# Weighted sums of modulation rows in a streaming-encoder block: products by ScalarE in place, sums by adding transfers on GpSimd's queue

## The chip, the cores and the metric

The kernel runs on one core of one Trainium2 chip. The metric is the device time of one execution in microseconds (us), here the median of three runs. The engines are TensorE (PE in the profile, PEld for its weight loads), VectorE (DVE), ScalarE (ACT), GpSimd (POOL) and SyncE (SP, which only issues transfers). Each takes its own list of instructions in order and waits at its head for semaphores of the others. 16 DMA engines move the data.

## The reference, cut to what matters

One residual block over x of 1024 tokens by 1024 channels: a mixer (four heads of a gated delta rule in chunks of 64, and a short gated convolution), then a SwiGLU, each behind a norm that a vector c modulates.

```python
c_act = jax.nn.silu(c)
mod = (c_act @ w_ada[l] + b_ada[l])[:, None, :]
shift1, scale1, gate1, shift2, scale2, gate2 = jnp.split(mod, 6, axis=-1)
h = rms_norm(x, norm1_w[l]) * (1.0 + scale1) + shift1
x = x + gate1 * hybrid_mixer(h, ...)
h = rms_norm(x, norm2_w[l]) * (1.0 + scale2) + shift2
x = x + gate2 * swiglu(h, w_gate[l], w_up[l], w_down[l])
return rms_norm(x, norm_f_w)
```

`w_ada` is 1024 by 6144, so `mod` is six rows of 1024 numbers. shift1 and scale1 (rows 0 and 1) are needed at the start and are made in another way. The late rows are 2 (gate1), 3 (shift2), 4 (scale2) and 5 (gate2); the change touches the sums of rows 2, 3 and 4, and the first product of row 5.

## The kernel before, in words

Everything is float32. Large matrix products are done as three float32r products of high and low parts, 128 by 128 weights times 128 by 512 data. The run has two parts. In the first, to about 470 us, all projections of the mixer, the delta rule and half of the output projection are made; in the second, the rest of the output projection and the SwiGLU (with a Strassen-like scheme).

The order of the first part is not written by hand. Every step is a task (`sim.spawn`, with a priority), and a planner (`class Sim`, L302) runs the tasks in a model of the engines with costs for each kind of instruction (`cost`, L371), takes at each point the task that could start first, and writes its instruction next. The result is one fixed list per engine. So a change of a cost or of an instruction gives another order for the whole of the first part from there on. Dense projections (`fill`, the tile `acc`) have the lowest priority and fill PE between the steps of the delta rule; their weights come through `raw` buffers and are split into parts `u`.

Late modulation rows are made by `ada_rows(b, ch)` (L988), one half row of 512 at a time. A half row has eight blocks kk of 128 rows of `w_ada`. For each block a buffer `raw` (there are five, shared with the loads of weights) is taken and loaded by SP, and VectorE multiplies it by the column kk of `c_act`, one number per partition, and adds it to `ac` (the tile `aacc`): a `tensor_scalar` for the first block (L998), a `scalar_tensor_tensor` for the seven others (L1000). What is left is a sum over the 128 partitions: `aacc` is split into a high and a low part (a cast by ScalarE or VectorE and a subtraction by VectorE), and two PE matmuls with a matrix of ones (the tile `ada`) put the sum into every partition of a PSUM bank.

`ada` (L1026) calls this for both halves of rows 2, 3 and 4, one after the other, without a buffer of its own (`get` is None, so `row` is true). There is one buffer `aacc`, so a half row begins when the one before has been split. For rows 3 and 4 the result is multiplied by an identity into `diag`, which uses the buffer of `aacc` too, and reduced to columns `mod_c`. `gate5` (L1015) makes row 5 later and passes buffers, so `row` is false there.

GpSimd has little to do in this part: per-head inverse roots (`rk`, `ro`), and the clearing of `A` (an array V that the recurrence of the delta rule fills: in each step matmuls `K`, `O` and `A`) before each of its steps.

Of the kernel before, what the change touches and what calls it, by code (L numbers as in the profile page):

```python
# [12 lines left out]
AF = mybir.ActivationFunctionType  # L13
ALU = mybir.AluOpType
# [37 lines left out]
def kernel(  # L52
# [25 lines left out]
    class Ordered:  # L78
# [18 lines left out]
    PE, DVE, ACT, POOL, SP = (Ordered(n, e) for n, e in (  # L97
        ("pe", nc.tensor), ("dve", nc.vector), ("act", nc.scalar), ("pool", nc.gpsimd), ("sp", nc.sync)))
# [7 lines left out]
    def nm(s):  # L106
        n_id[0] += 1
        return f"{s}_{n_id[0]}"

    xs, outs = x[0], out[0]  # L110
# [9 lines left out]
    class Banks:  # L120
# [3 lines left out]
        def get(self, name="ps"):  # L124
            b = self.ids[self.i % len(self.ids)]
            self.i += 1
            return psp.tile([P, HT], F32, name=nm(name), tag=f"b{b}")
# [61 lines left out]
    def dma(out, in_):  # L189
        SP.dma_start(out=out, in_=in_)  # L190
# [19 lines left out]
    c_act = cst.tile([P, KB], F32, name="c_act", tag="c_act")  # L210
# [91 lines left out]
    class Sim:  # L302
# [18 lines left out]
        def free(self, t):  # L321
            res, i = self.owner.pop(t.tensor.name)
            res.slots.append((max([a[4] for a in self.acc.get(t.tensor.name, [])] + [0.0]), i))
            res.slots.sort()
# [46 lines left out]
        def cost(self, eng, op, a, k):  # L371
            outs, ins = [], []
            pos = [v for v in a if hasattr(v, "tensor")]
            if "out" in k:
                outs.append(k["out"])
            else:
                outs.append(pos.pop(0))
            ins += pos
            for n, v in k.items():
                if n != "out" and hasattr(v, "tensor"):  # L380
                    (outs if n == "accum_out" else ins).append(v)
            o = outs[0]
            n = o.free_size()
            table = None
            if eng == "pe":
                if op == "transpose":
                    busy = 0.107
                else:
                    fast = ins[1].dtype == F32R
                    busy = max(n * 0.000443, 0.107) if fast else max(n * 0.00168, 0.224)  # L390
                lat = busy + 0.30
            elif op == "dma_start":
                busy, lat = 0.44, None
            elif eng == "act":
                big = max([n] + [v.free_size() for v in ins])
                busy = 0.15 + (0.1 if hasattr(k.get("scale"), "tensor") else 0.0) + big * 0.0007 + (0.19 if "accum_out" in k else 0.0)
                lat = busy + 0.25
                func = [v for v in a if isinstance(v, type(AF.Silu)) and v in (AF.Silu, AF.Exp, AF.Ln)] if op == "activation" else []
                if func:
                    table = str(func[0]).split(".")[-1]  # L400
            elif eng == "pool":
                busy = 1.1 if op == "tensor_tensor" else 0.5
                lat = busy + 0.15
            else:
                big = max([n] + [v.free_size() for v in ins])
                sb = all(v.space != PSUM for v in outs + ins)
                if op == "memset":
                    busy = 0.08 + n * 0.0005
                elif sb and op in ("tensor_copy", "tensor_scalar"):
                    busy = 0.08 + n * 0.00062  # L410
                else:
                    busy = 0.08 + big * 0.00104 + (0.05 if op == "scalar_tensor_tensor" else 0.0)
                if "accum_out" in k:
                    busy += 0.1
                lat = busy + 0.15
            return outs, ins, busy, lat, table
# [147 lines left out]
    def bank(res, name):  # L564
        return res.tile(psp, [P, HT], F32, name)

    def gt(tag, shape=(P, 4, P), dtype=F32):
        return GP[tag].tile(gp, list(shape), dtype, tag)

    def raw(shape=(P, HT), dtype=F32):  # L570
        return raws.tile(wst, list(shape), dtype, "raw")
# [10 lines left out]
    def esplit(src, hi, lo):  # L582
        ecopy(hi, src)
        DVE.tensor_tensor(lo, src, hi.bitcast(F32), ALU.subtract)

    def mm(out_, lhsT, rhs, start=True, stop=True):
        PE.matmul(out_, lhsT, rhs, start=start, stop=stop)
# [400 lines left out]
    def ada_rows(b, ch, ac=None, get=None):  # L988
        if ac is None:
            ac = wst.tile([P, HT], F32, name=nm("aacc"), tag="aacc", bufs=1)  # L990
        row = get is None
        get = get or raw
        c0 = b * D + ch * HT
        for kk in range(KB):
            r = get()
            dma(r, wada[kk * P:(kk + 1) * P, c0:c0 + HT])
            if kk == 0:
                DVE.tensor_scalar(ac, r, c_act[:, 0:1], None, ALU.mult)  # L998
            else:
                DVE.scalar_tensor_tensor(ac, r, c_act[:, kk:kk + 1], ac, ALU.mult, ALU.add)  # L1000
            free(r)
        hl = [raw(dtype=F32R) if row else gt("Tt", (P, HT), F32R) for _ in range(2)]
        esplit(ac, hl[0], hl[1])
        if not row:
            return hl
        ps = bank(chb, "ada")
        mm(ps, ones_r, hl[0], True, False)
        mm(ps, ones_r, hl[1], False, True)
        for t in hl:
            free(t)  # L1010
        return ps
# [3 lines left out]
    def gate5(ch):  # L1015
        sim.wait(lambda: len(us0) == KB and len(us1) == KB and "row" in done)
        if 5 not in gates:
            g = gates[5] = wst.tile([P, D], F32, name=nm("gate"), tag="gate", bufs=1)
            dma(g, b_ada[0, 5 * D:6 * D].partition_broadcast(P))
        ac = gt("A", (P, HT)) if ch else None  # L1020
        g5[ch] = ada_rows(5, ch, ac, (lambda: gt("Tt", (P, HT))) if ch else raw)
        done.add(("g5", ch))
        if ch:
            free(ac)

    def ada():  # L1026
        sim.wait(lambda: 1 in sc_)
        g = wst.tile([P, D], F32, name=nm("gate"), tag="gate", bufs=1)
        dma(g, b_ada[0, 2 * D:3 * D].partition_broadcast(P))
        for ch in range(2):  # L1030
            ps = ada_rows(2, ch)
            DVE.tensor_tensor(g[:, ch * HT:(ch + 1) * HT], g[:, ch * HT:(ch + 1) * HT], ps, ALU.add)
            free(ps)
        gates[2] = g
        for b in (3, 4):
            for ch in range(2):
                ps = ada_rows(b, ch)
                j = (b - 3) * 8 + ch * 4
                diag = wst.tile([P, 4, P], F32, name=nm("diag"), tag="aacc", bufs=1)
                DVE.tensor_tensor(diag, v3(ps, 4), bc1(ident, 4), ALU.mult)  # L1040
                free(ps)
                DVE.tensor_reduce(mod_c[:, j:j + 4], diag, mybir.AxisListType.X, ALU.add)
        DVE.tensor_tensor(mod_c, mod_c, bac[:, 24:40], ALU.add)
        DVE.tensor_copy(b2c, mod_c[:, 0:8])
        DVE.scalar_tensor_tensor(s2c, mod_c[:, 8:16], 1.0, n2c, ALU.add, ALU.mult)
        DVE.tensor_tensor(db2, b2c[:, 4:8], b2c[:, 0:4], ALU.subtract)
        done.add("mods")
# [1348 lines left out]
```

## Time and profile before

| what | value |
|---|---|
| median of three runs | 1159.26 us |
| range of the three runs | 1158.74 to 1159.27 us |
| profiled execution, first to last instruction (span) | 1158.3 us |
| PE, DVE, ACT, POOL busy in the span | 1148.2, 961.4, 565.6, 62.3 us |
| first and last start of a VectorE step on `aacc` | 113.0 and 465.8 us |
| DMA engines' busy share, 100 to 470 us | 0.49 |

Of the profiled execution its span is known; its own time is among the three runs, whose median lies 1.0 us above the span.

In the rows of groups the parts are: source line, engine, operation, the tile written and the tiles read, shapes, count, then busy time in us and the mean of one in ns, then the engine's idle time just before these instructions with what ended most of it. Nearly all instructions of the first part carry L448, the planner's line. In the rows of waits the numbers are us in total, times, and the longest. In the rows of the chain and of the timeline they are start and length in us. In the rows of DMA issues the last number is the median from issue to landing in us.

### The profile page before, as it was taken

What the parts mean: (1) busy time and instruction counts of PE and PEld (TensorE: products, weight loads), DVE (VectorE), ACT (ScalarE), POOL (GpSimd) and SP (SyncE); (2) the same over time, 40 slices, a digit from 0 to 9 for tenths busy, and PEclk for the clock granted to TensorE, in tenths of its full rate; (3) what the DMA queues carried; (4) which work ended last, traced back from release to release, by engine and by line L of the source; (5) the groups of instructions that cost most, each with busy time, mean ns of one, the idle gap of its engine ahead of it and who ended that gap; (6) DMA issues with size and microseconds to landing.
All of it is one profiled execution on the core that took longest, in us unless ns stands there. A gap on an engine that the chain in (4) does not pass through costs nothing.

```text
span 1158.3 us, 16873 instructions
## 1 busy us (share of the span) xinstructions
PE 1148.2 (99%) x5682; PEld 967.1 (83%) x5682; DVE 961.4 (83%) x1820; ACT 565.6 (49%) x1244; POOL 62.3 (5%) x100
## 2 busy tenths in 40 slices
PE   8999999999999999999999999999999999999997
PEld 7888888988888988888888888888888888888886
DVE  7899988999988898669987778877887798688676
ACT  6678732559634543346434443434434455443344
POOL 2110100001101001100000000000000000000002
PEclk9999999999999999999999999999999999999999
DMA  9824456534225546432564457545654599869403
GB/s 363 324 76 143 117 166 174 182 120 138 88 66 164 165 158 210 169 92 72 173 218 163 138 191 231 171 137 175 232 192 143 174 333 394 309 207 337 144 30 146
DMA packets 127544, 209.19 MB, mean 181 GB/s; under 512 B 20577, under 2 KB 45153, under 8 KB 127457
## 3 DMA queue, kind: packets, MB, share of 16 engines
q1 hardware_dynamic: 122080, 204.90, 52.8%
q10 hardware_dynamic: 5376, 3.21, 0.9%
q8 instruction: 45, 0.74, 0.3%
q14 instruction: 43, 0.34, 0.1%
HBM read 153.01 MB, written 55.05 MB: 180 GB/s over the span
## 4 chain that ended last, share of the span: by engine, by line
PE 94%; DVE 3%; ACT 1%; DMA 1%; issue 0%; ACTq 0%; DVEq 0%
PE acc L89 36%; PE acc L448 25%; PE dn L89 17%; PE o L89 4%; PE o L448 3%; PE tr L89 1%; PE K L448 1%; PE A L448 1%; DVE xo L90 1%; PE ab L448 1%; PE w L448 1%; PE u L448 1%; PE kk L448 1%; PE qk L448 1%; DMA raw<-in_w_out_dram 0%; DVE raw L448 0%
## 5 line engine op out<-in xcount | busy, mean ns | idle before, releaser
L448 PE MATMUL acc<-h,u 128*128 128x512 f32 x1200 | 297.9, 397 | 0.0
L448 PEld LDWEIGHTS acc<-h,u 128*128 128x128 f32 x1200 | 220.0, 188 | 42.5 <-issue 0.5
L89 PE MATMUL acc<-h,hl 128*128 128x512 f32 x576 | 135.1, 390 | 0.0
L89 PE MATMUL acc<-T,hl 128*128 128x512 f32 x552 | 130.8, 390 | 0.0
L89 PEld LDWEIGHTS acc<-h,hl 128*128 128x128 f32 x576 | 107.4, 188 | 21.9
L89 PEld LDWEIGHTS acc<-T,hl 128*128 128x128 f32 x552 | 102.4, 188 | 20.4
L90 DVE TENSOR_TENSOR xo<-xo,dn 128x512 f32<-128x512 f32 x84 | 57.0, 684 | 42.3 <-PE dn L89 34.6
L89 PE MATMUL acc<-h,u 128*128 128x512 f32 (+1 forms) x480 | 91.8, 341 | 0.0
L89 PE MATMUL dn<-h,h 128*128 128x512 f32 x396 | 90.7, 389 | 0.0
L89 PEld LDWEIGHTS acc<-h,u 128*128 128x128 f32 x480 | 78.3, 189 | 11.7
L89 PEld LDWEIGHTS dn<-h,h 128*128 128x128 f32 x396 | 74.3, 188 | 15.4
L90 DVE TENSOR_TENSOR cc<-cc,acc 128x512 f32<-128x512 f32 x66 | 41.4, 645 | 32.0 <-PE acc L89 32.0
L448 ACT CAST u<-raw 128x512 fp32r<-128x512 f32 x58 | 35.9, 621 | 56.9 <-PE acc L448 55.1
L448 DVE TENSOR_TENSOR u<-raw,u 128x512 fp32r<-128x512 f32 x82 | 56.1, 685 | 4.0 <-ACT u L448 3.5
L89 PE MATMUL acc<-T,u 128*128 128x512 f32 x240 | 56.0, 389 | 0.0
L448 DVE SCALAR_TENSOR_TENSOR cv<-pr,cols_a,cv 128x512 f32<-128x512 f32 x72 | 53.8, 756 | 0.3
L89 PEld LDWEIGHTS acc<-T,u 128*128 128x128 f32 x240 | 45.1, 188 | 9.3
L90 ACT CAST h<-rw 128x512 fp32r<-128x512 f32 x57 | 32.7, 618 | 41.3 <-PE dn L89 34.6
L90 ACT CAST hl<-S 128x512 fp32r<-128x512 f32 x44 | 25.3, 623 | 56.2 <-DVE S L90 56.2
L90 ACT ACTIVATE cc<-cc 128x512 f32<-128x512 f32 x33 | 20.9, 633 | 64.0 <-DVE cc L90 64.0
L90 ACT CAST u<-R 128x512 fp32r<-128x512 f32 (+1 forms) x60 | 34.2, 585 | 35.3 <-DVE R L90 34.2
L90 DVE TENSOR_TENSOR hl<-S,hl 128x512 fp32r<-128x512 f32 x44 | 28.5, 687 | 26.3 <-ACT hl L90 26.3
(377 smaller groups left out, 2145.1 us busy)
## 6 DMA issues: line engine op xcount, KB each, us to landing
raw<-in_w_in_dram SPq DMA_DIRECT2D x82, 256.0 KB, 3.3
am_scr<-cc SPq DMA_DIRECT2D x77, 256.0 KB, 4.3
raw<-in_w_ada_dram SPq DMA_DIRECT2D x56, 256.0 KB, 3.1
rw<-am_scr SPq DMA_DIRECT2D x55, 256.0 KB, 5.0
rw<-bm_scr SPq DMA_DIRECT2D x53, 256.0 KB, 5.1
bm_scr<-raw SPq DMA_DIRECT2D x51, 256.0 KB, 5.5
R<-in_w_gate_dram SPq DMA_DIRECT2D x22, 512.0 KB, 4.3
R<-in_w_up_dram SPq DMA_DIRECT2D x22, 512.0 KB, 5.5
```

The source lines that it names most:

```text
L89: return call(*a, **k)
L90: ins = call(*a, **k)
L448: ins = call(*a, **k)
```

## The change

For rows 2, 3 and 4, ScalarE multiplies each block in its own buffer by the column of `c_act`, and a transfer issued on GpSimd's queue then adds the buffer to `aacc` (the DMA engines read `aacc`, add and write it back). The first product, for all late rows, is made by ScalarE into `aacc`. Row 5 keeps VectorE's sums. The planner is told that such a transfer also reads its destination, and that it occupies GpSimd for 1.0 where it assumed 0.44 for every queue; that cost is the planner's own.

```diff
@@ cost
                 if n != "out" and hasattr(v, "tensor"):
                     (outs if n == "accum_out" else ins).append(v)
+            if "accum_op" in k:
+                ins.append(outs[0])
...
             elif op == "dma_start":
-                busy, lat = 0.44, None
+                busy, lat = (1.0 if eng == "pool" else 0.44), None
@@ ada_rows
             dma(r, wada[kk * P:(kk + 1) * P, c0:c0 + HT])
             if kk == 0:
-                DVE.tensor_scalar(ac, r, c_act[:, 0:1], None, ALU.mult)
+                ACT.activation(ac, r, AF.Copy, scale=c_act[:, 0:1])
+            elif row:
+                ACT.activation(r, r, AF.Copy, scale=c_act[:, kk:kk + 1])
+                POOL.dma_start(out=ac, in_=r, accum_op=ALU.add)
             else:
                 DVE.scalar_tensor_tensor(ac, r, c_act[:, kk:kk + 1], ac, ALU.mult, ALU.add)
             free(r)
```

The planner writes a new order from about 100 us on, and the lists meet again near the end of the first part; PE has the same matmuls in both. In the new program the source lines behind the edits are larger by 2 to 5 (L448 becomes L450).

GpSimd's list around the recurrence of the first half of the tokens, before (`A` is cleared whole once, then its upper half for three further steps; `qs` is scratch of the first step, `ro` an inverse root):

```order
L448 MEMSET A_2377 128x1024
L448 MEMSET qs_2383 64x512
L448 MEMSET A_2377 64x512 x3
L448 TENSOR_TENSOR ro_2827<-so_2823,nhalf 128x4
L448 TENSOR_TENSOR ro_2828<-so_2824,nhalf 128x4
```

and now:

```order
L450 MEMSET A_2278 128x1024
L450 MEMSET qs_2285 64x512
L450 DMA aacc_1919<-raw_2239 128x512
L450 MEMSET A_2278 64x512
L450 DMA aacc_2370<-raw_2375 128x512
L450 DMA aacc_2370<-raw_2398 128x512
L450 MEMSET A_2278 64x512
L450 DMA aacc_2370<-raw_2451 128x512
L450 DMA aacc_2370<-raw_2493 128x512
L450 MEMSET A_2278 64x512
L450 DMA aacc_2370<-raw_2544 128x512
L450 DMA aacc_2370<-raw_2587 128x512
```

The clearings that followed each other now have one or two transfers between them, each of which waits for the transfer before it.

PE's list at the fifth pair of `ada` matmuls, before (`A` and `K` belong to the recurrence, `acc` is a dense projection):

```order
L448 MATMUL A_509_2706<-S_456_2426,WQ_203_1013 128x128
L448 MATMUL acc_499_2661<-h3_1_140_761,u_478_2536 128x512
L448 MATMUL ada_510_2714<-raw_501_2664,ones_79 128x512
L448 MATMUL acc_499_2661<-h3_1_140_761,u_478_2536 128x512
L448 MATMUL acc_499_2661<-h4_1_145_787,u_482_2574 128x512 x3
L448 MATMUL acc_499_2661<-h5_1_147_793,u_482_2574 128x512
L448 MATMUL ada_510_2714<-raw_502_2665,ones_79 128x512
L448 MATMUL acc_499_2661<-h5_1_147_793,u_482_2574 128x512 x2
L448 MATMUL K_512_2724<-A_439_2377,kt_239_1212 128x128
```

and now:

```order
L450 MATMUL acc_716_3929<-h4_0_61_388,u_704_3870 128x512 x3
L450 MATMUL acc_716_3929<-h5_0_70_433,u_704_3870 128x512 x3
L450 MATMUL acc_716_3929<-h6_0_81_475,u_704_3870 128x512 x3
L450 MATMUL ada_721_3971<-raw_713_3924,ones_79 128x512
L450 MATMUL acc_716_3929<-h7_0_86_520,u_704_3870 128x512 x3
L450 MATMUL ada_721_3971<-raw_714_3925,ones_79 128x512
L450 MATMUL acc_723_3979<-h0_1_130_719,u_709_3900 128x512 x3
```

The fifth pair stood inside the recurrence of the first half of the tokens; it now stands in dense work behind it. All six pairs moved later and apart. Between the last matmul of one pair and the first of the next stand, of 512 wide instructions and of records of 128 wide ones (a float32 matmul leaves two records, a transpose one):

| stretch | before: wide, narrow | now: wide, narrow |
|---|---|---|
| first to second pair | 115, 28 | 139, 120 |
| second to third | 92, 0 | 150, 133 |
| third to fourth | 45, 104 | 182, 100 |
| fourth to fifth | 73, 104 | 182, 12 |
| fifth to sixth | 147, 69 | 209, 264 |

## The prediction

> **What bounds the kernel now.** I read the page's totals first, then the chain that ended last, then TensorE's own waits, and last the stage that the change touches.
>
> ```profile
> span 1158.3 us, 16873 instructions
> PE 1148.2 (99%) x5682; PEld 967.1 (83%) x5682; DVE 961.4 (83%) x1820; ACT 565.6 (49%) x1244; POOL 62.3 (5%) x100
> PE 94%; DVE 3%; ACT 1%; DMA 1%; issue 0%; ACTq 0%; DVEq 0%
> ```
>
> TensorE is busy for 99% of the span and holds 94% of the chain. A busy PE need not be PE at its peak, since the ends of matmuls are modelled, so I asked what PE waited for, and what its work costs by the start of one matmul to the next.
>
> ```profile
> PE heat L89 <- POOL nhalf L90: 1.4, 1, 1.4
> PE acc L448 <- ACT h L448: 1.4, 2, 0.9
> PE ps L89 <- DVE raw L90: 0.2, 1, 0.2
> PE y L448 <- DVE u L448: 0.2, 1, 0.2
> ...
> 151.49 0.89 PE qk L448 x8
> ...
> 153.51 19.54 PE acc L448 x86
> ```
>
> The first four rows are all of PE's waits in the whole run, 3.2 us, and only the last, 0.2 us, lies in the stage of the change. The two rows of the chain give the prices of records that follow each other without a wait: 19.54 / 86 = 0.227 us for a 512 wide one, 0.89 / 8 = 0.111 us for a 128 wide one. Now the stage from 100 to 470 us, where the late modulation rows are made:
>
> ```profile
> 100.00:470.00 370.00, 369.80 (x2004) 316.61 (x2003) 333.21 (x767) 196.17 (x551) 32.57 (x38) 1.00 0.49 150
> ...
> L448 PE MATMUL acc<-h,u 128*128 128x512 f32 x1045 | 260.8, 397 | 0.0
> L448 PE MATMUL o<-h,h 128*128 128x512 f32 x90 | 21.3, 390 | 0.0
> L448 PE MATMUL o<-wu,h 128*128 128x512 f32 x64 | 18.9, 399 | 0.0
> L448 PE MATMUL o<-L,h 128*128 128x512 f32 x32 | 10.7, 394 | 0.0
> L448 PE MATMUL ada<-raw,ones 128*128 128x512 f32 x12 | 5.0, 415 | 0.0
> L448 PE MATMUL row<-raw,ones 128*128 128x512 f32 x4 | 1.6, 395 | 0.0
> L448 PE MATMUL gbc<-qs,row_h 128*128 128x512 f32 x4 | 1.2, 410 | 0.0
> ```
>
> The wide records are 1045 + 90 + 64 + 32 + 12 + 4 + 4 = 1251, which leaves 753 narrow ones of the 2004. Their work is 1251 x 0.227 + 753 x 0.111 = 284.0 + 83.6 = 367.6 us. The stage lasts 370. So PE loses some 2.4 us in it, with the granted clock at 1.00, and that is all that any change to other engines can win here.
>
> **The change, part by part.** *Off VectorE.*
>
> ```profile
> L448 DVE SCALAR_TENSOR_TENSOR aacc<-raw,c_act,aacc 128x512 f32<-128x512 f32 x42 | 31.2, 742 | 1.4 <-DMA raw<-in_w_ada_dram 1.3
> L448 DVE TENSOR_SCALAR aacc<-raw,c_act 128x512 f32<-128x512 f32 x6 | 3.1, 522 | 0.5 <-DMA raw<-in_w_ada_dram 0.4
> ```
>
> The 42 multiply-adds of the six half rows go, 31.2 us, and so do their six first products, 3.1 us (and two more of the last row): 34.3 us of VectorE in the stage. VectorE was busy for 333 of the 370 us, but PE stood almost nowhere behind it, so this is worth at most PE's 2.4 us. I take nothing of it: those gaps are where the written order fits the chip badly, and an order written anew will have gaps of its own, more or fewer by about 1 us.
>
> *Onto ScalarE.* 48 products by a column in the stage (and two later). The nearest row is its multiplication by a tap's column:
>
> ```profile
> L448 ACT ACTIVATE cv<-pr,cols_a 128x512 f32<-128x512 f32 x12 | 8.8, 730 | 0.9 <-DVE pr L448 0.6
> ```
>
> That is 48 x 0.73 = 35 us more on an engine that is busy for 196 of 370; it is covered by its idle time. ScalarE executes in order, so a product whose load is late holds what stands behind it.
>
> *Onto GpSimd's queue and the DMA engines.* 42 transfers of 256 KB from `raw` into `aacc`. Each must wait until the one before has landed, since both change `aacc`, and GpSimd stands still in that wait. The trace shows no such transfer, so I bound one, from GpSimd's release to the landing, by 256 KB transfers of the other queues:
>
> ```profile
> raw<-in_w_ada_dram SPq DMA_DIRECT2D x48, 256.0 KB, 3.0
> z_scr<-zs SPq DMA_DIRECT2D x7, 256.0 KB, 2.2
> y_scr<-cv SPq DMA_DIRECT2D x3, 256.0 KB, 2.0
> ...
> bm_scr<-raw SPq DMA_DIRECT2D x51, 256.0 KB, 5.5
> ...
> L448 POOL MEMSET A<- 128x1024 f32 x4 | 3.8, 954 | 105.4 <-DVE raw L448 51.4 <-DMA dx<-A 44.7 <-PE Q L448 9.3
> ```
>
> Low end 2.0 us, a store out of SBUF in this stage. High end 5.5 us, the slowest 256 KB group of SBUF stores, plus about 1 us for an engine that makes the request by software (taken from GpSimd's plain memset, 0.95): 6.5. I take 4.2: the 2.0 of the store in this stage, 1.0 for GpSimd, and 1.2 for the second stream, since the destination has to be read as well and the DMA engines are already 49% busy. This is an estimate, and the weakest number here.
>
> The Trainium skill, "DMA: Bandwidth & Descriptors", section "Anatomy of one DMA — SWDGE (gpsimd) path", fits a transfer of GpSimd's queue by 2.0 us plus bytes over 436 GB/s, 2.6 us for this size before the second read; no row here shows one. By it the sum below stays as it is.
>
> *What room they have.* The six pairs of `ada` matmuls stand in PE's queue, and PE takes it in order, so a late sum stops PE there. In the written order the stretches between one pair and the next were 115, 92, 45, 73 and 147 wide instructions with 28, 0, 104, 104 and 69 narrow records; they become 139, 150, 182, 182 and 209 wide with 120, 133, 100, 12 and 264 narrow. At 0.227 and 0.111 that was 29, 21, 22, 28 and 41 us of PE work, and is 45, 49, 52, 43 and 77 us. The tightest is ahead of the fifth pair: 43 us. In it fall the work on the fourth pair, whose scratch shares the buffer of `aacc`, the first product, seven transfers and the first cast:
>
> ```profile
> L448 DVE TENSOR_TENSOR diag<-ada,ident 128x512 f32<-128x512 f32 x4 | 2.7, 683 | 0.0
> L448 DVE TENSOR_REDUCE mod_c<-diag 128x4 f32<-128x512 f32 x4 | 2.7, 679 | 0.0
> L448 ACT CAST u<-raw 128x512 fp32r<-128x512 f32 x44 | 27.4, 622 | 53.6 <-PE acc L448 53.4
> ```
>
> 0.68 + 0.68 + 0.73 + 0.62 = 2.7, so seven transfers have 40 us, 5.7 each; with hand-overs between engines call it 5.5. Ahead of the second pair no scratch is in the way and (45 - 1.35) / 7 = 6.2. At 4.2 us seven take 29.4, and 10 us are to spare at the tightest place. Loads that wait for a buffer which a transfer still reads have the same room to lose, as the five `raw` buffers are shared with the weights. The cover that hides all of it is PE's dense work; without it seven transfers would show 29 us for each half row.
>
> *New heads of queues.* The cast behind the last transfer of a half row now holds ScalarE or VectorE until that lands. Before, it waited as well:
>
> ```profile
> ACT raw L448 <- DVE aacc L448: 4.5, 3, 4.2
> ```
>
> Three waits there, 4.5 us together and the longest 4.2, have no counterpart among PE's waits. I put 0.5 us for all six.
>
> *The sum.* PE's work is the same, 0; gaps 0 (from -2.4 to +1); new heads +0.5. On the profiled span that is 1158.3 + 0.5 = 1158.8. The runs' median, 1159.26, lies 1.0 above the span, so I forecast **1159.8 us**. A measurement of this kernel can tell about 0.2%, 2.3 us, from no change, and the forecast lies within that.
>
> **The rivals.** *Slow transfers (slower, 0.27).* The point from which it decides is 5.5 us for one. Then seven outlast the dense work ahead of the fifth pair, and above 6.2 ahead of the second too. At the high end, 6.5, the price is 7 x 1.0 + 7 x 0.3 = 9 us: 1159.8 + 9 = 1169. For it: a software queue and a second read, and the 5.5 us stores. Against it: those stores run in a later stage, while stores in this one take 2.0 to 2.2.
>
> The Trainium skill, "SBUF — State Buffer", warns of a "DVE blocks DMA" trap: GpSimd can't write its descriptors while VectorE copies fp32 within SBUF in a two-port mode. Here such a copy or cast lasts some 0.4 us and there are few, so it would lengthen a transfer now and then and not decide; no run here shows it.
>
> *GpSimd is held when the recurrence needs it (slower, 0.10).* Its clearing of the upper half of `A` (the array V) stands between `O` and the next `K` in each step:
>
> ```profile
> 222.93 0.89 PE O L448 x8
> ...
> 227.02 0.89 PE K L448 x8
> ...
> 223.94 0.52 POOL L448 MEMSET A<- 64x512 f32 x1 [16.81 <-PE O L448]
> ```
>
> It ends at 224.46 and `K` starts at 227.02, 2.6 us later. In the new order pairs of transfers stand between the memsets. If the second of a pair still waits for the first when `O` ends, the clearing comes late by up to one transfer, 4.2 - 2.6 = 1.6 us, in each of up to four such steps: up to 6.4 us, typically half, 1159.8 + 3.2 = 1163. Against it: a step lasts about 11 us and two transfers 8.4.
>
> *VectorE's relief shows (faster, 0.05).* If all gaps of the stage close and nothing new opens, 1159.26 - 2.4 = 1156.9. For it only that VectorE was 90% busy; against it, that PE waited 0.2 us in the stage.
>
> *The change does nothing at all* can be excluded from the written order: the 42 transfers stand in GpSimd's queue.
>
> **How the numbers follow.** The forecast has 0.58, the slow rivals 0.37, the fast one 0.05. Within the forecast I see 1157.5 to 1161.5. The range reaches up to 1168, which leaves out only the longest transfers (about 0.08), and down to 1157.5, which leaves out about 0.04 and the mishaps that I haven't named.
>
> **What would show it.** In the new profile: the `aacc` multiply-adds of VectorE reduced to the 7 of each half of the last row; GpSimd's DMA rows, 42 of 256 KB, with a landing time under 5.5 us; PE's waits with no row for `ada` above 1 us; VectorE's busy time some 35 us lower and the span the same. A row "PE ada <- ACT raw" or "<- DVE raw" of several us would mean slow transfers; a row "PE K <- POOL A" the held GpSimd. A time under 1157 would mean that I misread PE's gaps.

## The result and the profile after

| | before | after |
|---|---|---|
| median of four runs each | 1159.26 us | 1173.42 us |
| range | 1158.74 to 1159.68 | 1173.12 to 1174.13 |
| ratio, 95% interval | | 1.0121 [1.0107, 1.0136] |

The change costs 14.2 us, above the range of 1157.5 to 1168. The page of the new profile, span, busy times and chain:

```profile
span 1171.3 us, 17005 instructions
PE 1151.4 (98%) x5682; PEld 967.8 (83%) x5682; DVE 938.3 (80%) x1774; ACT 594.1 (51%) x1290; POOL 97.1 (8%) x142
PE 92%; DMA 4%; DVE 2%; ACT 1%; issue 1%; POOL 0%; SPq 0%; DVEq 0%; ACTq 0%; POOLq 0%
```

VectorE was relieved (961 to 938 us) and the end came later. The DMA share of the chain rose from 1% to 4%: transfers are now on the path. PE's waits in the stage, total, times and longest, show where:

```profile
PE y L450 <- DVE u L450: 4.3, 2, 3.8
PE ada L450 <- ACT raw L450: 2.9, 1, 2.9
PE K L450 <- DVE A L450: 1.4, 1, 1.4
PE A L450 <- DVE S L450: 0.9, 2, 0.6
```

Before, this list held one row of 0.2 us; now it holds 9.5 us. The transfers in the same stage (first their queue as a whole: packets, MB, share of 16 engines; then the median landing):

```profile
q0 software_dynamic: 6048, 11.01, 17.6%
...
raw<-in_w_ada_dram SPq DMA_DIRECT2D x54, 256.0 KB, 3.5
aacc<-raw POOLq DMA_DIRECT2D x42, 256.0 KB, 4.3
```

The 4.3 us run from a transfer's issue to its landing. The prediction's 4.2 us ran from GpSimd's release, so the way from a landing to the next issue belongs to it as well. The chain of waits ahead of the fifth `ada` pair, start and length, shows that way:

```profile
347.31 5.67 DMA aacc<-raw
...
353.63 5.61 DMA aacc<-raw
...
359.89 4.42 DMA aacc<-raw
...
364.40 0.63 ACT raw L450
...
365.07 0.50 PE ada L450
```

Here a transfer lands after 4.4 to 5.7 us, and the next is issued about 0.65 us later. So what the prediction put at 4.2 us is 4.3 + 0.65 = 4.95 us by the median, and 5.1 to 6.3 us here. What stands ahead of the first of the seven transfers is in the lists of PE, ScalarE and GpSimd (two `ada` matmuls, the first of them the last of the fourth pair):

```profile
319.14 0.40 PE L450 MATMUL ada<-raw,ones 128*128 128x512 f32 x1
...
324.24 0.71 ACT L450 ACTIVATE aacc<-raw,c_act 128x512 f32<-128x512 f32 x1
...
326.13 0.72 ACT L450 ACTIVATE raw<-raw,c_act 128x512 f32<-128x512 f32 x1 [0.43 <-DMA raw<-in_w_ada_dram]
...
327.26 0.91 POOL L450 DMA_DIRECT2D aacc<-raw  x1 [11.64 <-ACT jk L450]
...
365.07 0.50 PE L450 MATMUL ada<-raw,ones 128*128 128x512 f32 x1 [2.86 <-ACT raw L450]
```

PE's dense work between the pairs ends at 365.07 - 2.86 = 362.21 us, 43 us behind the fourth pair, just as predicted. But 8.1 us of it pass before the first transfer is issued, where the prediction had 2.1 for the scratch and the first product. ScalarE takes the first product only behind other steps of its list (`jk`, for which it waited 1.57 us for PE), and the first transfer needs the second product too, which waits 0.43 us for its load. The seven transfers last from 327.26 to the landing at 364.31, 37.05 us or 5.3 each. With 8.1 us ahead of them and 0.8 behind them for the cast, 34.2 us were left, 4.9 each, and PE waits 2.9 us. Next the chain in the second recurrence:

```profile
404.06 5.43 DMA aacc<-raw
...
409.54 3.04 DMA raw<-in_w_out_dram
...
412.70 0.69 DVE raw L450
...
413.42 0.69 DVE A L450
```

A load of `w_out` starts 0.05 us after a transfer has released its `raw` buffer, VectorE multiplies it 0.1 us after it has landed, and the step on `A` for which `K` waits stands behind that in VectorE's list. SP, which issues the loads, waits 22.9 us for such releases between 380 and 450 us:

```profile
SPq L450 <- DMA aacc<-raw: 22.9, 6, 4.5
```

The largest wait has another look. PE's timeline at `y`, and below it the stretches behind the wait (the number after POOL's is the granted clock):

```profile
436.14 0.63 PE L450 MATMUL y<-ident,u 128*128 128x128 f32 x4
436.52 0.47 PE L450 MATMUL o<-wu,h 128*128 128x512 f32 x1
440.76 1.12 PE L450 MATMUL y<-ident,u 128*128 128x128 f32 x4 [3.76 <-DVE u L450]
442.45 1.09 PE L450 MATMUL y<-ident,u 128*128 128x128 f32 x4 [0.57 <-DVE u L450]
```

```profile
440.00:442.00 2.00, 1.12 (x4) 0.71 (x4) 1.10 (x3) 0.00 (x0) 1.58 (x1) 0.50 1.10 268
442.00:444.00 2.00, 1.55 (x6) 1.48 (x7) 1.93 (x4) 1.54 (x3) 0.00 (x0) 0.50 1.04 415
444.00:446.00 2.00, 2.00 (x6) 1.53 (x6) 1.84 (x4) 0.84 (x2) 0.00 (x0) 0.53 0.83 315
446.00:448.00 2.00, 2.00 (x11) 1.65 (x10) 2.00 (x4) 0.00 (x0) 0.00 (x0) 1.00 0.06 5
```

Between the second and the third group of `y` the new order gives PE one 512 wide instruction of `o`, and then nothing. The 4.3 us of waiting are followed by 6 us at half clock: PE is busy for 4.7 of them and does half the work in that time, so some 2.3 us more are lost, 6.6 in all. The stage's waits and this clock are 9.5 + 2.3 = 11.8 of the 14.2 us; the rest is not located.

### The profile page after: what moved, and what is told of

Read it like the earlier page. It is cut to its first block, busy times and chain, and to the rows that moved or that the text cites. A ratio compares the mean times of both kernels' runs of the same rounds, so it can differ in the third digit from the quotient of the medians.

```text
span 1171.3 us, 17005 instructions
## 1 busy us (share of the span) xinstructions
PE 1151.4 (98%) x5682; PEld 967.8 (83%) x5682; DVE 938.3 (80%) x1774; ACT 594.1 (51%) x1290; POOL 97.1 (8%) x142
## 3 DMA queue, kind: packets, MB, share of 16 engines
q0 software_dynamic: 6048, 11.01, 5.6%
## 4 chain that ended last, share of the span: by engine, by line
PE 92%; DMA 4%; DVE 2%; ACT 1%; issue 1%; POOL 0%; SPq 0%; DVEq 0%; ACTq 0%; POOLq 0%
PE acc L89 36%; PE acc L450 23%; PE dn L89 17%; PE o L89 4%; PE o L450 3%; DMA aacc<-raw 3%; PE tr L89 1%; PE K L450 1%; PE A L450 1%; DMA wa<-in_w_mod_dram 1%; DVE xo L90 1%; PE ab L450 1%; PE w L450 1%; PE u L450 1%; PE kk L450 1%
## 5 line engine op out<-in xcount | busy, mean ns | idle before, releaser
L450 PE MATMUL acc<-h,u 128*128 128x512 f32 x1200 | 301.0, 398 | 0.0
L450 PEld LDWEIGHTS acc<-h,u 128*128 128x128 f32 x1200 | 219.2, 188 | 42.0 <-issue 0.5
L89 PE MATMUL acc<-h,hl 128*128 128x512 f32 x576 | 135.1, 390 | 0.0
L89 PE MATMUL acc<-T,hl 128*128 128x512 f32 x552 | 130.8, 390 | 0.0
L89 PEld LDWEIGHTS acc<-h,hl 128*128 128x128 f32 x576 | 107.4, 188 | 21.9
L89 PEld LDWEIGHTS acc<-T,hl 128*128 128x128 f32 x552 | 102.4, 188 | 20.4
L89 PE MATMUL acc<-h,u 128*128 128x512 f32 (+1 forms) x480 | 91.8, 341 | 0.0
L89 PE MATMUL dn<-h,h 128*128 128x512 f32 x396 | 90.7, 389 | 0.0
L89 PEld LDWEIGHTS acc<-h,u 128*128 128x128 f32 x480 | 78.3, 189 | 11.7
L89 PEld LDWEIGHTS dn<-h,h 128*128 128x128 f32 x396 | 74.3, 188 | 15.4
L450 ACT CAST u<-raw 128x512 fp32r<-128x512 f32 x66 | 40.8, 620 | 55.6 <-PE acc L450 53.0
L450 DVE TENSOR_TENSOR u<-raw,u 128x512 fp32r<-128x512 f32 x82 | 56.1, 686 | 12.1 <-ACT u L450 11.4
L89 PE MATMUL acc<-T,u 128*128 128x512 f32 x240 | 56.0, 389 | 0.0
L450 DVE SCALAR_TENSOR_TENSOR cv<-pr,cols_a,cv 128x512 f32<-128x512 f32 x72 | 54.0, 758 | 0.6
L450 POOL DMA_DIRECT2D aacc<-raw x42 | 37.0, 881 | 193.3 <-ACT raw L450 54.9
L89 PEld LDWEIGHTS acc<-T,u 128*128 128x128 f32 x240 | 45.0, 188 | 9.4
L90 POOL TENSOR_SCALAR fst<-fst 128x1 f32<-128x1 f32 x8 | 3.3, 410 | 592.1 <-ACT jf L90 592.1
```

The lines of the kernel that those rows point to most:

```text
L89: return call(*a, **k)
L90: ins = call(*a, **k)
L450: ins = call(*a, **k)
```

## The experiments

The first question was how much belongs to the transfers and how much to what else the change does. **a_dve_add**: products by ScalarE in place, but the sums by VectorE.

```diff
-                POOL.dma_start(out=ac, in_=r, accum_op=ALU.add)
+                DVE.tensor_tensor(ac, ac, r, ALU.add)
```

> The products stay with ScalarE in place, the 42 sums go back to VectorE as plain adds (no transfer of GpSimd's queue at all). The change took 1173.4 us, before 1159.3. Theory A (transfers last longer from one to the next than the written order leaves room for, and what waits behind them comes late): without them the time is that of before within 3 us, 1157 to 1162. Theory B (ScalarE's products wait for loads at the head of its queue and hold its other work): the loss stays, 1168 or more. Theory C (the transfers' traffic slows the other loads) says the same as A here.

1161.90 us (1161.29 to 1162.95), ratio 1.0021 [1.0012, 1.0031]: within A's range. ScalarE's products, with an order of their own, cost 2.4 us and no more; the rest comes only where the sums are made by transfers, in the order that goes with them.

**b_true_cost**: the changed kernel, and the planner counts an adding transfer 1.8 us longer.

```diff
                     end = rd = self.pipe + DMA_T[1]
+                    if eng == "pool":
+                        end = rd = end + 1.8
```

> The change as it is, only that the planner counts each adding transfer 1.8 us longer, as the trace of the changed kernel shows it (4.3 us to landing and some 0.6 until the next is issued), so that it writes another order with more room. Theory A: most of the 14 us come back, 1159 to 1164. Theories B (ScalarE's products hold its queue) and C (traffic) have the same products and transfers: 1170 or more.

1175.20 us, ratio 1.0134 [1.0117, 1.0151]: nothing came back, against A. The time lies in the range of B and C, of which a_dve_add speaks against B only. PE's waits from 100 to 560 us:

```profile
PE row L89 <- ACT Tt L450: 6.6, 1, 6.6
PE tr L89 <- DVE raw L90: 2.0, 2, 1.3
PE tr L89 <- DVE x L450: 1.2, 2, 0.9
PE tr L89 <- ACT raw L90: 0.9, 1, 0.9
...
```

The waits at the fifth pair and at `y` are gone, as A says, and others of 10.7 us stand at the hand-over to the second part: `row` on L89 is row 5's sum, `tr` the first transposes of the second norm. A plan that knows the length only moved the loss.

**c_short**: exactly the changed kernel's order on all engines, each transfer cut to 128 of 512 columns. **f_plain**: the same order, whole transfers that overwrite instead of adding. Their edits, one after the other:

```diff
+            if "accum_op" in k:
+                k = dict(k, out=k["out"][:, 0:128], in_=k["in_"][:, 0:128])
...
+            if "accum_op" in k:
+                k = {n: v for n, v in k.items() if n != "accum_op"}
             ins = call(*a, **k)
```

> Exactly the order of the change on every engine, but each of the 42 transfers adds only the first 128 of 512 columns (so three quarters of the sums are left out). Theory A: transfers land in 3.3 us or less where 4.3 were, and most of the loss goes, 1160 to 1165. Theory B (ScalarE's products) and a theory D that the new order is bad by itself: 1172 to 1174, since nothing on ScalarE or in the order changes. Theory C (traffic) would also give back time, and the landings of the loads from HBM would go back from 3.5 to 3.0 us.

> Exactly the order of the change, but the 42 transfers overwrite their destination and don't add (so the sums are left out, only the last block stays). What does the adding cost? My estimate of a transfer had 1.2 us for the second read. If it is that: landing 3.1 us instead of 4.3, and by theory A the time falls to 1162 to 1166. If the software queue is what costs: landing 4.2 us and 1172 to 1174.

1166.68 us, ratio 1.0060 [1.0045, 1.0075], and 1166.73 us (1166.17 to 1167.16), ratio 1.0061 [1.0046, 1.0076]. Landings, c_short's row first, then f_plain's queue and row:

```profile
aacc<-raw POOLq DMA_DIRECT2D x42, 64.0 KB, 2.8
```

```profile
q0 software_dynamic: 3360, 11.01, 7.8%
...
aacc<-raw POOLq DMA_DIRECT2D x42, 256.0 KB, 3.3
```

Both times lie a little above A's ranges, by 1.7 and 0.7 us, and far below those of its rivals; f_plain's landing is 3.3 where 3.1 was expected. Two quite different transfers give the same time. **p_no_transfer** tells why: the same order with none at all.

```diff
+            if "accum_op" in k:
+                return None
             ins = call(*a, **k)
```

> The changed kernel's order without any adding transfer (GpSimd's 42 transfers are left out, so of each sum only the first block is made; ScalarE's products stay). Theory 'written order': the half of the loss that short transfers did not give back lies in the new order itself, in which VectorE has more to do behind the second recurrence than PE has work to cover, first seen at y and, with y moved apart, at the hand-over to the second part. Expected 1165 to 1167.5 us, with PE's wait for u at y still 3 us or more. Rival 'rest of the transfers': what stayed is the 2.8 us that a short transfer still takes and GpSimd's time for it; expected 1159 to 1162 us.

1166.82 us, ratio 1.0059 [1.0044, 1.0074], in the range of 'written order'. Transfers that land in 3.3 us are as good as none, and those that land in 4.3 cost 1173.42 - 1166.73 = 6.7 us over the 42 (7.0 by the ratios). The other 7 us are in the written order itself, without a transfer. PE's waits in this run, and below them the slices behind the longest:

```profile
PE y L452 <- DVE u L452: 4.0, 2, 3.5
PE A L452 <- DVE S L452: 0.2, 1, 0.2
```

```profile
434.00:436.00 2.00, 1.15 (x5) 0.78 (x6) 1.10 (x3) 0.68 (x2) 1.09 (x1) 0.50 1.05 419
436.00:438.00 2.00, 2.00 (x7) 1.81 (x8) 1.77 (x4) 1.37 (x3) 0.00 (x0) 0.50 0.78 269
438.00:440.00 2.00, 2.00 (x6) 1.52 (x6) 2.00 (x4) 0.43 (x1) 0.00 (x0) 0.50 0.23 85
```

So the waits at the fifth pair and at `K` belong to the whole adding transfers, and that at `y` to the order. The wait of 4.0 us at `y` and 2.6 us lost at half clock behind it (half of PE's 5.15 us there) are nearly all of the order's 7 us. How much of the transfers' 6.7 us comes by way of their traffic (theory C) and not by their landings is not separated: the loads of `w_ada` land in a median of 3.5 us in the changed kernel, 3.2 in c_short, and 3.3 in f_plain and in p_no_transfer. **l_short_fifth** and **m_short_sixth** cut only the fifth or the sixth half row's transfers.

```diff
+        cut[0] = b == 4 and ch == 0
...
+            if "accum_op" in k and cut[0]:
+                k = dict(k, out=k["out"][:, 0:128], in_=k["in_"][:, 0:128])
```

> The changed kernel's order; only the seven transfers of the fifth half row (first half of row 4) are cut to 128 of 512 columns, three quarters of that sum left out. Theory 'two costs': the wait of 2.9 us at the fifth ada pair goes and PE is that much earlier in what follows; expected 1169 to 1171.5 us. Rival: what sets the end is the sixth half row's hold on buffers and the y transposes, which the fifth pair's wait runs beside; expected 1172.5 to 1174 us.

> The same for the sixth half row alone (second half of row 4). Theory 'two costs': the loads of w_out behind the held buffers come in time, PE's lag grows by some 4 us less between PE work 400 and 422 us; the wait at the fifth pair and that at y stay; expected 1168.5 to 1171 us. Rival, that the holds on buffers are a wait beside another one: 1172.5 to 1174 us.

1169.20 us, ratio 1.0089 [1.0073, 1.0104], and 1171.86 us, ratio 1.0101 [1.0086, 1.0116]. By the ratios the fifth half row gives back 1.0121 - 1.0089 = 0.32%, 3.7 us, within the range of 'two costs'. The sixth gives 2.3 us, between the two ranges, and its interval overlaps with the changed kernel's, so its share isn't settled. Of l's four runs three took 1169.0 to 1169.3 us; the profiled one took 1172.69, and it has no wait at the fifth pair but one of 2.2 us at the first, which the changed kernel's profile has not.

Then the order. **g_y_apart** moves `y` apart by telling the planner that the inverse roots of the second half come 3 us later; **h_short_y_apart** does so with c_short's transfers.

```diff
                 lat = busy + 0.15
+                if o.tensor.name.startswith("ro") and ("chain", 1) in done:
+                    lat += 3.0
```

> The planner is told that the inverse roots ro of the second half of the tokens come 3 us later, and nothing else is changed; the order is that of the changed kernel up to PE work position 419 us, and behind it the four groups of y transposes stand at 424.6, 426.1, 431.7 and 434.6 instead of 421.7, 422.6, 423.3 and 423.7. Theory 'two costs': the late landings cost about half of the 14 us, and the other half is the written order at y, where PE has no other work between ro, u and y, waits 4.3 us and then runs on at half clock. Expected 1165.5 to 1168.5 us, PE's wait for u under 1 us. Rival 'one cost': the wait at y is only where the buffers that the transfers hold show last, and would show at the next matmul; expected 1171 to 1175 us.

> Both at once: the y transposes apart as in the run before, and every adding transfer moves 128 of 512 columns (three quarters of the sums are left out). Theory 'two costs': the two add up, 1159 to 1162 us. Rival 'one cost': nothing beyond what the short transfers gave, 1165.5 to 1168 us.

1176.31 us (1173.11 to 1177.63), ratio 1.0139 [1.0122, 1.0155], and 1167.19 us, ratio 1.0061 [1.0044, 1.0078]. The first lies above both ranges, the second in that of 'one cost'. My theory of two costs at two places fell: the wait at `y` went and nothing was won. The rows of h show where it went:

```profile
PE tr L89 <- DVE raw L90: 1.9, 2, 1.2
PE tr L89 <- DVE x L454: 1.8, 2, 0.9
PE tr L89 <- ACT raw L90: 0.9, 1, 0.9
```

The same hand-over as in b_true_cost. Something that feeds it is late, and the order pays at `y` or there. Two candidates: VectorE's amount of work, or the late rows themselves. **r_less_dve** leaves out VectorE's sixteen products of `w_out` by the gate row, in p_no_transfer's order; **s_before_less_dve** does it to the kernel before, **t_less_dve_full** to the changed one.

```diff
-            DVE.tensor_tensor(r, r, gates[2][:, cs], ALU.mult)
+            sim.either([("dve", "tensor_tensor", lambda *a, **k: None, (r, r, gates[2][:, cs], ALU.mult), {})])
```

> The changed kernel's order without its adding transfers, as in the run without transfers, and besides VectorE's sixteen products of w_out by the gate row are left out (16 instructions of about 0.69 us, 11 us, most of them issued between the second recurrence and y); nothing else moves. Theory 'VectorE's backlog': the wait at y (4.0 us there) falls under 1 us and nothing takes its place, 1159 to 1161.5 us. Rival 'chain of latencies' (the inverse roots of GpSimd and the steps behind them follow each other however little VectorE has to do): 1164.5 to 1167 us with the wait still there.

> Control: the same sixteen products left out of the kernel before, nothing else moved. PE stands nowhere behind VectorE in its first part, so both theories expect 1158 to 1160 us. If it gains 3 us or more, taking work from VectorE is worth something by itself and the run before it says less.

> The same sixteen products left out of the changed kernel, with all 42 adding transfers whole. Theory 'VectorE's backlog': what the held buffers cost goes mostly by the same way (late w_out loads hold VectorE), only the wait at the fifth ada pair stays, about 3 us: 1161 to 1165 us. Rival, that the transfers' half has its own way to PE: only the order's half comes back, 1166 to 1168 us.

1164.91 us, ratio 1.0045 [1.0030, 1.0060]; 1158.95 us, ratio 0.9995 [0.9985, 1.0004]; 1170.97 us, ratio 1.0090 [1.0073, 1.0107]. Eleven us less for VectorE give under 2 us in the first, within the range of the chain of latencies, nothing that can be told in the control, and 2.4 us by the medians in the last (3.6 by the ratios), less than either theory expected there. In r the wait stands:

```profile
PE y L452 <- DVE u L452: 3.1, 1, 3.1
```

Since that order has nothing else for PE at that place, the candidates were tried where `y` stands apart. **u_row_free** starts from h and lets the `row` matmuls (made by `mod_rows` from scale2) go without the late rows; **w_apart_less_dve** starts from h and leaves out VectorE's sixteen products.

```diff
-        sim.wait(lambda: "mods" in done and ("gdn", 1) in done)
+        sim.wait(lambda: ("gdn", 1) in done)
...
-            DVE.tensor_tensor(dg, bc1(ident, 4), bc2(s2c[:, 4 * ch:4 * ch + 4], P), ALU.mult)
+            DVE.tensor_tensor(dg, bc1(ident, 4), bc2(n2c[:, 4 * ch:4 * ch + 4], P), ALU.mult)
```

> Short transfers (three quarters of the sums left out), y apart, and the row matmuls no longer wait for the late rows: they use the norm's own weights in place of scale2's column, so that the scale is left out of them. The order changes behind y only, row 5 can begin before the sixth ada pair. Theory 'late sixth pair': the hand-over is set by the chain from the sixth pair through row and row 5, so 1160 to 1164 us. Rival 'VectorE's amount of work': 1165.5 to 1168 us, with PE's waits for x and raw at the transposes still there.

> Short transfers, y apart, the row matmuls waiting as before, and VectorE's sixteen products of w_out by the gate row left out (11 us, with no other change of order). Rival 'VectorE's amount of work': 1159.5 to 1163 us. Theory 'late sixth pair': 1165 to 1167.5 us, since the chain's own steps are as long as before.

1162.16 us, ratio 1.0023 [1.0014, 1.0033], and 1165.15 us, ratio 1.0051 [1.0036, 1.0066]. Both fall into the ranges of the theory "late sixth pair". PE's waits from 100 to 560 us, in u and then in w:

```profile
PE o L454 <- DVE h L454: 1.3, 1, 1.3
...
```

```profile
PE tr L89 <- DVE raw L90: 1.8, 2, 1.1
PE tr L89 <- DVE x L454: 1.3, 2, 0.9
PE tr L89 <- ACT raw L90: 0.9, 1, 0.9
```

With `row` free, the waits at the hand-over are gone and 5 of the order's 7 us with them (4.4 by the ratios). The order behind `y` is another one in u too, with the first `row` matmul at 452.1 us instead of 455.2. The `ada` matmuls, of before and of the changed kernel (first and last start at the end of the row's times):

```profile
L448 PE MATMUL ada<-raw,ones x12: 392/395/478, 141.1 to 292.3; 128*128 128x512 f32 x12
```

```profile
L450 PE MATMUL ada<-raw,ones x12: 387/395/504, 165.7 to 455.4; 128*128 128x512 f32 x12
```

The last one came at 292 us, and `mod_c` was ready long before the recurrence's end. Now it comes at 455 (at 449 in h_short_y_apart). Behind it stands a chain: columns `mod_c`, `row`, the sums of row 5 (which wait for `row`), the second norm, its transposes. Before, only the recurrence's end fed that chain.

Last, whole kernels whose planner knows the length (1.8 us more). **q_rows34_true** uses transfers for rows 3 and 4 only, **i_rows23_true** for rows 2 and 3 only; **j_first_act** is the kernel before with the first product alone by ScalarE.

```diff
-            elif row:
+            elif row and b > 2:
```

> A whole kernel: row 2 keeps VectorE's sums, rows 3 and 4 use the adding transfers (28 of the 42), and the planner counts each 1.8 us longer, near what was measured. This is the order, of the divisions tried on paper, in which the planner's own model leaves PE without a stretch of idling and ends VectorE's list least behind that of the kernel before (1 us). Theory 'written order': with 28 slow transfers, 14 of them beside the second recurrence, but an order that knows their length, 1159.5 to 1163 us and no wait of PE above 1 us in the stage. Rival 'the transfers of row 4 disturb the second recurrence whatever the order': 1166 to 1171 us.

> The other division: rows 2 and 3 by adding transfers (28), row 4 by VectorE, counted 1.8 us longer too. Here the planner's own model ends VectorE's list some 4 us behind that of the kernel before. Theory 'written order': 1162.5 to 1166 us though no transfer runs beside the second recurrence, with the loss at y or at the hand-over. Rival 'row 4's transfers': 1159 to 1162 us.

> The kernel before with one part of the change alone: the first product of each half row by ScalarE, no transfers. It also gives a new order, with its own small differences. Both theories: 1159 to 1161.5 us; it shows what an order written anew costs without the transfers.

1162.82 us, ratio 1.0025 [1.0016, 1.0035]; 1162.28 us, ratio 1.0027 [1.0015, 1.0039]; 1161.56 us, ratio 1.0012 [1.0003, 1.0021]. q lies at the upper end of the range of 'written order' and far below its rival's. But it does not test that rival, against its expectation: its last transfer is issued at 381.6 us, just as GpSimd begins to clear `A` for the second recurrence, whose steps `K` run from 386.7 to 421.6, so 27 of its 28 transfers stand ahead of that. In the changed kernel six are issued beside those steps or behind them. i lies between the two ranges and tells nothing apart by its time. Its profile, of its slowest run (1165.37 us), does: with the last pair already at 430.8 us PE waits 3.2 us at the transposes of the hand-over, and there the chain goes through a late `y` (452.7) and `row` (457.9). So a late last pair is one way to these waits and not the only one. j is 0.1 us above its range. For q, the landings and the only wait of PE from 100 to 560 us:

```profile
aacc<-raw POOLq DMA_DIRECT2D x28, 256.0 KB, 4.4
```

```profile
PE P L450 <- DVE qs L450: 0.5, 1, 0.5
```

28 transfers of 4.4 us hide wholly, in an order that leaves them room and has the last pair at 391.5 us. By the medians q is 2.8 us, i 2.3 and j 1.5 behind the kernel before on the same chip. i's waits at the hand-over are seen in its slowest run only; for q and j, with 0.5 us and no waits of PE from 100 to 560 us, it stays open where the time goes. No version beat the kernel before.

## Why the prediction was wrong

- *Nothing to win* held. PE's gaps were put at 2.4 us, and 11 us of work taken off VectorE in the kernel before won nothing that can be told (s_before_less_dve).
- *4.2 us for a transfer*, from GpSimd's release to the landing, was 0.75 us short: 0.65 from one landing to the next issue and 4.3 from there to the landing. The part for the second read was near (1.2 put, 1.0 measured).
- *"At 4.2 us seven take 29.4, and 10 us are to spare at the tightest place"* failed. The 43 us of dense work were right. What was set against them was not: 8.1 us pass ahead of the first transfer where 2.1 were put, and the seven transfers take 37.05 us where 29.4 were put, with landings of up to 5.7 us in just that stretch. With the cast that is 45.9 us against 43, the wait of 2.9 us. The point from which a transfer decides was set at 5.5 us; with 8.1 us ahead it lies at 4.9, and the 5.3 measured are above the one and below the other. In whole runs, landings of 3.3 us lose nothing (f_plain) and landings of 4.3 lose 6.7 us.
- *"Loads that wait for a buffer which a transfer still reads have the same room to lose"* failed. Such a load has only the time until VectorE reaches its product, and the recurrence's steps stand behind that in VectorE's list: waits of 1.4 us at `K` and 0.9 at `A`, of which p_no_transfer has 0.2.
- *Gaps of the new order, "more or fewer by about 1 us"* is the step that failed most: 7 us, shown by p_no_transfer without any transfer. In the changed kernel's order they are the wait at `y` and the half clock behind it. With `y` moved apart the loss stands at the hand-over, and u_row_free, in an order of its own behind `y`, gives most of it back when `row` need not wait for the late rows. I measured the room between the six pairs and never what stands behind the sixth, though the same table said that each pair moves later: its last matmul starts 163 us later and now feeds `row`, row 5 and the hand-over. Whether the late sixth pair is also why the planner draws `y` together is not shown: no run frees `row` in that order.
- The rival *slow transfers* had the right first place (the wait of `ada` for ScalarE's cast) and a wrong point; it is one half of the loss, 6.7 us where its price was 9. The rival *GpSimd held* did not come: `K` waits for VectorE's `A`, never for GpSimd.
- A price for the clock was missing as well: 2.3 us behind the wait at `y`.

## What to carry to other kernels

When a chain of steps becomes slower but still fits between its own consumers, follow it past the last one: ask what the end of the chain feeds, and whether that used to be ready for long. Where an order is planned, try the new order with the suspected operation shortened and with it left out; what stays is the order's. Compare the room with a whole step, hand-over and slowest landings included, not with the median of the transfer, and take off what stands ahead of the first step.

## What the runs showed of the hardware

An adding transfer is not free on the DMA engines. With the same bytes, adding takes 6048 packets where overwriting takes 3360, 17.6% of the 16 engines' time in the stage against 7.8%, and lands in 4.3 us against 3.3. The Trainium skill, "Collectives: The Full Stack", section "Stop ④ — SDMA + CCE: where bytes move and the add happens", describes the addition in the DMA path as read, read and write "with the add free in between". These rows agree with more being moved than in an overwriting transfer; the addition with its second read costs 1.0 us for 256 KB here.

A wait of PE of some 3 us can halve its clock, by the clock records of these traces for 3.4 or 6.8 us each time. Behind 3.76 us at `y` (above) it was 6.8 us, behind 3.51 there in f_plain 3.4. At the fifth pair a wait of 2.9 us left the clock at 1.00 in the changed kernel's profile, halved it for 3.4 us in m_short_sixth's, and for 6.8 us in g_y_apart's (the rows below). In h_short_y_apart's three waits of 0.75 to 1.17 us within 9 us at the hand-over were followed by 3.4 us at half clock.

The slices of g_y_apart, the granted clock behind POOL's number:

```profile
366.00:368.00 2.00, 1.80 (x4) 1.49 (x5) 1.69 (x3) 0.95 (x3) 1.73 (x4) 0.50 0.35 131
...
370.00:372.00 2.00, 2.00 (x6) 1.52 (x6) 1.12 (x3) 0.00 (x0) 0.00 (x0) 0.50 0.76 256
372.00:374.00 2.00, 2.00 (x13) 1.76 (x12) 0.15 (x1) 0.62 (x1) 0.00 (x0) 0.96 0.69 239
```

The Trainium skill, "TensorE: Matmul & The Clock Gate", section "What's actually happening", puts the clock at half rate after an idle window of about 3.4 us that runs free of the kernel. The lengths of 3.4 and 6.8 us agree with such a window. That a wait of 2.9 us sometimes suffices differs from it; the rows decide.
